# Seven block products for every two feed-forward units: the up-projections of a two-block float32 model as Strassen-Winograd products, with their outputs parked in DRAM

## The chip, the cores and the metric

The kernel is one program on one NeuronCore of a Trainium2 chip. The engines that matter are TensorE (PE in the profile), VectorE (DVE), ScalarE (ACT) and GpSimd (POOL); SyncE (SP) issues nearly all DMAs. The metric is the device time of one execution. Three runs of the kernel before took 3021.39 to 3023.06 us, median 3022.3 us.

## The reference

Two model blocks run one after the other on 1024 tokens of width 1024, all in float32. Each has a mixer part and then a feed-forward part with a residual sum. Only the feed-forward parts are changed:

```python
h = h + swiglu(rmsnorm(h, norm_ffn[i]), w_gate[i], w_up[i], w_down[i])   # first block, 2816 wide
#   swiglu: (silu(h @ w_gate) * (h @ w_up)) @ w_down
h = rmsnorm_2(x, g_ffn[i])                                               # second block, 4096 wide
x = x + jnp.square(jax.nn.relu(h @ w_ffn_up[i])) @ w_ffn_down[i]
```

The three matrices `w_gate`, `w_up` and `w_ffn_up` are the up-projections, `w_down` and `w_ffn_down` the down-projections. Below, FFN1 is the feed-forward part of the first block and FFN2 that of the second.

## The kernel before

**Numbers.** A float32 product is made of three TensorE products: each operand is split into a high part (a cast to fp32r, by ScalarE) and a low part (operand minus high part, by VectorE), and `mm3` (L139, L140, L141) adds high by high, high by low and low by high in PSUM. One such matmul has a 128x128 weight tile and 512 moving columns. The split is `split` (L103 ScalarE, L104 VectorE).

**Units.** 128 columns of an up-projection are a unit: 22 in FFN1, for gate and for up, and 32 in FFN2. The weights of a unit are one 512 KB tile, 128x1024: eight 128x128 tiles along the inner dimension k. Its output, 128 columns by 1024 tokens, fills one PSUM tile `big` of two banks, one for each half of the tokens; there are four of these tiles. A unit takes 8 k-tiles by 2 halves by 3 = 48 matmuls.

**Order of `ffn` (L639).** `norm_t` scales the residual rows and transposes them on TensorE (L192) into `hn`, 16 pairs of a high and a low half that stay in SBUF; `norm_units` does the first half of the tokens, starts the first units on it, and does the second half behind them. Then for each unit: product, activation (`swiglu` L664: Silu on ScalarE L667, product on VectorE L668; `relu2` L671: L674, L675), and the split of the result into `a` (L122, L124). After every third unit (four in FFN1's last chunk, two in FFN2's) `tok_matmul` multiplies the three `a` by their three rows of the down-projection, and VectorE adds each of the eight 128x1024 results to the residual tile (L659), which stays in SBUF. So up and down work alternate, and nothing of it goes through DRAM.

**What sets the order.** Each engine has one instruction stream, which a scheduler lays out when the program is built; an engine takes its instructions strictly in that order, and one that waits holds back all behind it. Tiles come from pools: 38 slots `S` of 128x1024 for all long-lived data, two buffers each for raw weights `wr`, split weights `wh` and `wl` and activations `zo`, and the four `big` in PSUM. The waits are made per tile: work on one half of a `big` tile waits for an earlier reader of its other half too.

## Time and profile before

| | us |
|---|---|
| median of three runs | 3022.3 |
| the profiled execution | 3025.18 |
| its span | 3023.3 |
| PE busy / DVE busy / ACT busy / POOL busy | 2899.8 / 1404.1 / 825.3 / 21.8 |

The span is the stretch in which the engines ran; the profiled execution is 1.9 us longer, and 2.9 us above the median of the runs. FFN1 begins with the transposes at 311.23 us and lasts until about 1050 us, FFN2 begins at 2191.8 us and lasts until 2917 us. Busy time of matmuls overlaps: a matmul is listed with 0.39 to 0.40 us and the next begins 0.23 us after its start, so the count of matmuls in a window says more than their sum.

### The profile page before, as it was taken

The numbers are of one execution on the slowest core, as the hardware profiler recorded it, in microseconds if no ns is written. First come the engines' busy times: TensorE is split into PE (matmuls) and PEld (weight loads), VectorE is DVE, ScalarE is ACT, GpSimd is POOL, SyncE is SP. The second block draws the span as 40 slices with busy tenths as digits, with TensorE's granted clock in tenths as the row PEclk, the third lists the DMA queues.
The fourth block names the chain that finished last, engine by engine and source line by source line (L and its number), as shares of the span: only waits on it lengthen the run. The fifth ranks groups of instructions, "written<-read, shape, count | busy, mean of one in ns | idle before, by whom it ended". The sixth has DMA issues, their size and how long they took to land.

```text
span 3023.3 us, 36716 instructions
## 1 busy us (share of the span) xinstructions
PE 2899.8 (96%) x15289; PEld 2327.6 (77%) x15289; DVE 1404.1 (46%) x2469; ACT 825.3 (27%) x1229; POOL 21.8 (1%) x73
## 2 busy tenths in 40 slices
PE   8989999999999999989788999999999999999998
PEld 6777888888888877867566777777888888888877
DVE  7774422222222462276676436545453333333366
ACT  4242311211121344143342334432131221111142
POOL 0000000000000000000000000000000000000000
PEclk9999999999999998999899999999999999999999
...
GB/s 133 105 128 146 35 42 42 63 44 40 42 63 49 73 137 153 105 117 90 69 90 88 98 83 13 29 105 134 75 35 42 42 56 49 56 49 42 42 77 98
DMA packets 126390, 225.37 MB, mean 75 GB/s; under 512 B 52177, under 2 KB 73297, under 8 KB 126225
## 3 DMA queue, kind: packets, MB, share of 16 engines
...
## 4 chain that ended last, share of the span: by engine, by line
PE 87%; DVE 9%; issue 2%; ACT 1%; DMA 1%; ACTq 0%; SPq 0%; DVEq 0%
PE big L139 24%; PE big L140 24%; PE big L141 24%; PE big L822 2%; PE chain L855 2%; DVE tt L1145 2%; DVE wt L1144 2%; PE ps L839 1%; PE ps L1114 1%; PE ps L1021 1%; PE big L192 1%; PE chain L1205 0%; PE chain L139 0%; PE chain L140 0%; PE chain L141 0%
## 5 line engine op out<-in xcount | busy, mean ns | idle before, releaser
L139 PE MATMUL big<-hn,wh 128*128 128x512 f32 x1872 | 745.6, 399 | 8.5 <-DVE zo L914 4.0
L141 PE MATMUL big<-hn,wl 128*128 128x512 f32 x1872 | 742.5, 397 | 5.3 <-DVE wl L104 5.2
L140 PE MATMUL big<-hn,wh 128*128 128x512 f32 x1872 | 744.5, 398 | 1.9 <-DVE hn L197 1.9
L139 PEld LDWEIGHTS big<-hn,wh 128*128 128x128 f32 x1872 | 352.8, 189 | 94.2 <-issue 6.2
L141 PEld LDWEIGHTS big<-hn,wl 128*128 128x128 f32 x1872 | 353.4, 189 | 90.7 <-DVE wl L104 8.4
L140 PEld LDWEIGHTS big<-hn,wh 128*128 128x128 f32 x1872 | 353.0, 189 | 88.0 <-issue 3.2
L103 ACT CAST wh<-wr 128x1024 fp32r<-128x1024 f32 (+1 forms) x142 | 141.9, 1000 | 966.4 <-PE big L140 777.4
L104 DVE TENSOR_TENSOR wl<-wr,wh 128x1024 fp32r<-128x1024 f32 (+1 forms) x142 | 165.0, 1162 | 410.5 <-ACT wh L103 405.7
L140 PE MATMUL big<-wk,a 128*128 128x512 f32 x864 | 338.4, 394 | 0.0
L141 PE MATMUL big<-wk,a 128*128 128x512 f32 x864 | 338.3, 393 | 0.0
L139 PE MATMUL big<-wk,a 128*128 128x512 f32 x864 | 334.9, 396 | 1.8 <-ACT wk L103 1.8
L659 DVE TENSOR_TENSOR r<-big,r 128x1024 f32<-128x1024 f32 x144 | 176.2, 1224 | 318.2 <-PE big L141 318.1
L139 PEld LDWEIGHTS big<-wk,a 128*128 128x128 f32 x864 | 160.9, 188 | 43.8 <-ACT wk L103 7.6
L140 PEld LDWEIGHTS big<-wk,a 128*128 128x128 f32 x864 | 162.2, 188 | 38.8 <-DVE wk L104 0.7
L141 PEld LDWEIGHTS big<-wk,a 128*128 128x128 f32 x864 | 162.2, 188 | 37.6
L674 ACT ACTIVATE zo<-big 128x1024 f32<-128x1024 f32 x32 | 32.8, 1026 | 371.4 <-PE big L141 371.4
L668 DVE TENSOR_TENSOR zo<-zo,big 128x1024 f32<-128x1024 f32 x22 | 26.9, 1221 | 205.2 <-PE big L141 205.2
L104 DVE TENSOR_TENSOR wk<-wr,wk 128x1024 fp32r<-128x1024 f32 (+1 forms) x86 | 100.3, 1171 | 31.1 <-ACT wk L103 31.0
L140 PE MATMUL big<-wk,mx 128*128 128x512 f32 x256 | 102.3, 399 | 1.3 <-DVE wk L104 1.3
L139 PE MATMUL big<-wk,mx 128*128 128x512 f32 x256 | 101.0, 401 | 2.3 <-ACT wk L103 2.3
L141 PE MATMUL big<-wk,mx 128*128 128x512 f32 x256 | 101.6, 397 | 0.0
L675 DVE TENSOR_TENSOR zo<-zo 128x1024 f32<-128x1024 f32 x32 | 39.2, 1225 | 131.7 <-ACT zo L674 131.7
...
## 6 DMA issues: line engine op xcount, KB each, us to landing
wr<-in_w_ffn_up_dram SPq DMA_DIRECT2D x32, 512.0 KB, 3.2
wr<-in_w_ffn_down_dram SPq DMA_DIRECT2D x32, 512.0 KB, 3.2
zr<-zo SPq DMA_DIRECT2D x24, 512.0 KB, 3.5
wr<-in_w_gate_dram SPq DMA_DIRECT2D x22, 512.0 KB, 3.3
wr<-in_w_up_dram SPq DMA_DIRECT2D x22, 512.0 KB, 3.2
wr<-in_w_down_dram SPq DMA_DIRECT2D x22, 512.0 KB, 3.2
wr<-in_w_gates_dram SPq DMA_DIRECT2D x16, 512.0 KB, 4.9
gd<-zo SPq DMA_DIRECT2D x16, 512.0 KB, 3.0
```

Of the source, the lines that this page charges most:

```text
L103: nc.scalar.copy(hi, x)
L104: nc.vector.tensor_tensor(lo, x, hi.bitcast(F32), ALU.subtract)
L139: nc.tensor.matmul(ps, lhsT=w[0], rhs=x[0], start=start, stop=False)
L140: nc.tensor.matmul(ps, lhsT=w[0], rhs=x[1], start=False, stop=False)
L141: nc.tensor.matmul(ps, lhsT=w[1], rhs=x[0], start=False, stop=stop)
L659: nc.vector.tensor_tensor(res[t], ps, res[t], ALU.add)
L674: nc.scalar.activation(s, ps, AF.Relu)
L675: nc.vector.tensor_tensor(s, s, s, ALU.mult)
L822: nc.tensor.matmul(sc[:, c:c + m], lhsT=qs[e][:, i * P:(i + 1) * P], rhs=ks[e][:, c:c + m], start=True, stop=True)
L855: nc.tensor.matmul(o, lhsT=pts[t // 4][:, (t % 4) * P:(t % 4 + 1) * P], rhs=vh, start=t == 0, stop=t == i)
L1144: nc.vector.tensor_tensor(t3, d[h, j:j + 1, j + 1:32].to_broadcast([64, n, m]), tt[h, 0:n, j:j + 1].to_broadcast([64, n, m]), ALU.mult)
L1145: nc.vector.tensor_tensor(tt[h, 0:n, j + 1:32], tt[h, 0:n, j + 1:32], t3, ALU.add)
```

## The change

For every two units j and j+1 of an up-projection, call the k-tiles 0 to 3 and 4 to 7 of their weights A11, A12 (unit j) and A21, A22 (unit j+1), and the two halves of k by the two halves of the tokens of the normed input B11, B12, B21, B22. The Strassen-Winograd scheme makes the four output blocks from seven products of four k-tiles each, 7 x 4 x 3 = 84 matmuls where two units took 96.

- `norm_blocks` makes B11, B21, B22 and the sums T1 to T4 of the input blocks, each split in high and low parts, once per feed-forward part; they stay in 28 of the 38 slots.
- `pair_weights` loads two units, makes the sums S1 to S4 of the weights with four GpSimd additions, and splits A11 with A12, S1 with S2, S3 with S4, and A22.
- `pair_steps` does the seven products in halves of two `big` tiles; p1, p5, u2 and u3 are partial sums in SBUF, and three copies on ScalarE, four additions on VectorE and one on GpSimd combine them.
- `ffn` does all pairs first, with the activation of each written to a DRAM tensor `hd`, and the residual to `rd`; afterwards it loads the residual, the activations and the down-projection again and does all chunks of the down-projection one after the other (a first chunk of one unit in FFN1, of two in FFN2, then three each: eight chunks for seven, and eleven as before).

```diff
+    def norm_blocks(self, res, g, groups=(3, 1)):
+        nc = self.nc
+        x = {n: [None] * 4 for n in ("B11", "B21", "B22", "T1", "T2", "T3", "T4")}
+        plain = [None] * 4
+        def norm_half(half):
+            xs, t = [], 4 * half
+            for n in groups:
+                xs += self.scaled(res[t:t + n])
+                t += n
+            for k in range(4):
+                ps = self.big()
+                for j in range(2):
+                    for i in range(4):
+                        c = (4 * j + i) * P
+                        nc.tensor.transpose(ps[:, c:c + P], xs[i][:, (k + 4 * j) * P:(k + 4 * j + 1) * P], self.ident)
+                p1, p2 = self.halves(ps)
+                g1, g2 = self.col(g, k), self.col(g, k + 4)
+                if half == 0:
+                    plain[k] = self.slot("bf")
+                    for n, p, c, f in (("B11", p1, g1, plain[k][:, 0:H]), ("B21", p2, g2, plain[k][:, H:2 * H])):
+                        x[n][k] = hi, lo = self.half_pair("hn")
+                        nc.scalar.activation(hi, p, AF.Identity, scale=c)
+                        nc.vector.tensor_scalar(f, p, c, None, ALU.mult)
+                        nc.gpsimd.tensor_tensor(lo, f, hi.bitcast(F32), ALU.subtract)
+                    continue
+                b12, t12, t34 = self.slot("tf")[:, 0:H], self.slot("tf"), self.slot("tf")
+                t1, t2, t3, t4 = *self.halves(t12), *self.halves(t34)
+                nc.scalar.activation(b12, p1, AF.Identity, scale=g1)
+                nc.gpsimd.tensor_tensor(t1, b12, plain[k][:, 0:H], ALU.subtract)
+                x["B22"][k] = hi, lo = self.half_pair("hn")
+                nc.scalar.activation(hi, p2, AF.Identity, scale=g2)
+                nc.vector.scalar_tensor_tensor(lo, p2, g2, hi.bitcast(F32), ALU.mult, ALU.subtract)
+                nc.vector.scalar_tensor_tensor(t3, p2, g2, b12, ALU.mult, ALU.subtract)
+                nc.vector.scalar_tensor_tensor(t2, p2, g2, t1, ALU.mult, ALU.subtract)
+                nc.gpsimd.tensor_tensor(t4, plain[k][:, H:2 * H], t2, ALU.subtract)
+                for t, names in ((t12, ("T1", "T2")), (t34, ("T3", "T4"))):
+                    hi, lo = self.slot("hn", F32R), self.slot("hn", F32R)
+                    self.split(t, hi, lo)
+                    for n, h, l in zip(names, self.halves(hi), self.halves(lo)):
+                        x[n][k] = h, l
+        return x, norm_half
+    def pair_weights(self, src):
+        nc = self.nc
+        raw = [self.wp.tile([P, 1024], F32, tag="wr", name=self.nm("wr"), bufs=2) for _ in range(2)]
+        for r, s in zip(raw, src):
+            nc.sync.dma_start(r, s)
+        a11, a12, a21, a22 = *self.halves(raw[0]), *self.halves(raw[1])
+        w = {}
+        def put(x, *names):
+            hi, lo = self.slot("wc", F32R), self.slot("wc", F32R)
+            self.split(x, hi, lo)
+            for n, h, l in zip(names, self.halves(hi), self.halves(lo)):
+                w[n] = h, l
+        put(raw[0], "A11", "A12")
+        yield w
+        s12, s34 = (self.wp.tile([P, 1024], F32, tag=t, name=self.nm("ws"), bufs=2) for t in ("wh", "wl"))
+        s1, s2, s3, s4 = *self.halves(s12), *self.halves(s34)
+        nc.gpsimd.tensor_tensor(s1, a21, a22, ALU.add)
+        nc.gpsimd.tensor_tensor(s2, s1, a11, ALU.subtract)
+        put(s12, "S1", "S2")
+        nc.gpsimd.tensor_tensor(s3, a11, a21, ALU.subtract)
+        nc.gpsimd.tensor_tensor(s4, a12, s2, ALU.subtract)
+        put(s34, "S3", "S4")
+        w["A22"] = self.half_pair("wc")
+        self.split(a22, *w["A22"])
+        yield w
+    def pair_steps(self, weights, x, c1, c2):
+        nc = self.nc
+        def product(ps, a, b, start):
+            for k in range(4):
+                self.mm3(ps, tuple(v[:, k * P:(k + 1) * P] for v in w[a]), x[b][k], start and k == 0, k == 3, skip_group_check=True)
+        w = next(weights)
+        pa, pb = self.halves(self.big())
+        p1 = self.slot("pr")[:, 0:H]
+        product(pa, "A11", "B11", True)
+        nc.scalar.copy(p1, pa)
+        product(pb, "A12", "B21", True)
+        nc.vector.tensor_tensor(c1[:, 0:H], pb, p1, ALU.add)
+        yield
+        next(weights)
+        pc, pd = self.halves(self.big())
+        p5 = self.slot("pr")[:, 0:H]
+        u2, u3 = self.halves(self.slot("pr"))
+        product(pc, "S1", "T1", True)
+        nc.scalar.copy(p5, pc)
+        product(pa, "S2", "T2", False)
+        nc.scalar.copy(u2, pa)
+        product(pd, "S3", "T3", True)
+        nc.vector.tensor_tensor(u3, pd, u2, ALU.add)
+        product(pc, "S4", "B22", False)
+        nc.vector.tensor_tensor(c1[:, H:2 * H], pc, u2, ALU.add)
+        nc.gpsimd.tensor_tensor(c2[:, H:2 * H], u3, p5, ALU.add)
+        product(pd, "A22", "T4", False)
+        nc.vector.tensor_tensor(c2[:, 0:H], pd, u2, ALU.add)
+        yield
+    def ffn(self, res, g, nf, chunks, up, act, w_down, last=lambda: None):
+        nc = self.nc
+        rd = self.dp.tile([T, D], F32, name=self.nm("rd"))
+        hd = self.dp.tile([nf, P, T], F32, name=self.nm("hd"))
+        for t in range(8):
+            nc.sync.dma_start(rd[t * P:(t + 1) * P, :], res[t])
+        x, norm_half = self.norm_blocks(res, g)
+        norm_half(0)
+        for j in range(0, nf, 2):
+            outs = []
+            for i, u in enumerate(up):
+                w = self.pair_weights((u[j], u[j + 1]))
+                c = [self.zo() if i == 0 else self.slot("cu") for _ in range(2)]
+                outs.append(c)
+                st = self.pair_steps(w, x, *c)
+                if j == 0 and i == 0:
+                    next(st)
+                    norm_half(1)
+                for _ in st:
+                    pass
+            for i in range(2):
+                act(*(c[i] for c in outs))
+                nc.sync.dma_start(hd[j + i], outs[0][i])
+        res = self.load_res(rd)
+        f = 0
         for nch in chunks:
             acts, wd = [], []
             for _ in range(nch):
-                if first:
-                    ps, first = first[:nu], first[nu:]
-                else:
-                    ps = [self.unit_t(ws.pop() if ws else self.weights(u[f]), hn) for u in up]
-                acts.append(act(*ps))
+                h = self.weights(hd[f], keep=True)
+                acts.append([tuple(v[:, half * H:half * H + H] for v in h) for half in range(2)])
                 wd.append(self.weights(w_down[f * P:(f + 1) * P, :], keep=True))
                 f += 1
             def evac(t, ps):
                 nc.vector.tensor_tensor(res[t], ps, res[t], ALU.add)
-                if t == 3 and f == sum(chunks):
+                if t == 3 and f == nf:
                     last()
             self.tok_matmul(acts, wd, evac)
...
+    def swiglu(self, g, u):
+        nc = self.nc
+        nc.scalar.activation(g, g, AF.Silu)
+        nc.vector.tensor_tensor(g, g, u, ALU.mult)
+
+    def relu2(self, h):
+        self.nc.vector.scalar_tensor_tensor(h, h, 0.0, h, ALU.max, ALU.mult)
 
...
-        self.ffn(res, "norm_ffn", (3, 3, 3, 3, 3, 3, 4), (a["w_gate"], a["w_up"]), self.swiglu, a["w_down"], self.ple_inputs)
+        res = self.ffn(res, "norm_ffn", FF1, (1,) + (3,) * 7, (a["w_gate"], a["w_up"]), self.swiglu, a["w_down"], self.ple_inputs)
-        self.ffn(res, "g_ffn_2", (3,) * 10 + (2,), (a["w_ffn_up"],), self.relu2, a["w_ffn_down"])
+        res = self.ffn(res, "g_ffn_2", FF2, (2,) + (3,) * 10, (a["w_ffn_up"],), self.relu2, a["w_ffn_down"])
```

What stands in the engines' streams now, at three places. A row is line, operation, what it writes and reads; the number behind a name is the buffer's, and the bracket names the engine or DMA queue whose semaphore it waits for.

ScalarE in the middle of FFN1, before: one unit pair of gate and up, where `big` is the finished gate product, `wh` and `wk` are weights of later work, `zo` the activation and `a` its high half.

```order
L103 CAST wh_3952<-wr_3950 128x1024 [waits DMAHW2_49,PE_49,Activation_49]
L667 ACTIVATE zo_3935<-big_3831 128x1024 [waits PE_49]
L103 CAST wh_4007<-wr_4005 128x1024 [waits DMAHW3_49,DVE_49,PE_49]
L122 ACTIVATE a_3938<-zo_3935 128x512 [waits DVE_49]
L122 ACTIVATE a_3939<-zo_3935 128x512
L103 CAST wk_3946<-wr_3944 128x1024 [waits DMAHW1_49]
```

ScalarE at the same place now, from the end of the gate pair to the up pair (`big_2968` and `big_3013` hold the gate pair, `big_3092` and `big_3137` the up pair; `zo_2958` and `zo_2959` are the two gate outputs, `pr` the partial sums, `ws` and `ws_3121` the sums of weights).

```order
L739 COPY pr_3014<-big_3013 128x512 [waits DVE_49,PE_49,Activation_49]
L741 COPY pr_3015<-big_2968 128x512 [waits DVE_49,PE_49]
L103 CAST wc_3088<-wr_3084 128x1024 [waits DMAHW0_49,Activation_49]
L795 ACTIVATE zo_2958<-zo_2958 128x1024 [waits DMAHW1_49,DVE_49]
L795 ACTIVATE zo_2959<-zo_2959 128x1024 [waits DMAHW2_49,DVE_49,Pool_49]
L730 COPY pr_3093<-big_3092 128x512 [waits PE_49,Activation_49]
L103 CAST wc_3124<-ws_3120 128x1024
L103 CAST wc_3130<-ws_3121 128x1024 [waits Activation_49]
L103 CAST wc_3134<-wr_3085 128x512 [waits DMAHW3_49,Activation_49]
```

The evacuation of p1 of the up pair (`pr_3093`) stands behind the two Silus, the second of which waits for VectorE's and GpSimd's parts of the gate pair; the cast of the next weight sums (`wc_3124`) stands behind it.

TensorE in the same up pair: the end of the product S3 T3 in one half of `big_3137` (with `hn_2738`) and the beginning of S4 B22 in its other half (with `hn_2644`).

```order
L139 MATMUL big_3137<-hn_2738,wc_3130 128x512
L140 MATMUL big_3137<-hn_2739,wc_3130 128x512
L141 MATMUL big_3137<-hn_2738,wc_3131 128x512
L139 MATMUL big_3137<-hn_2644,wc_3130 128x512 [waits DVE_49]
L140 MATMUL big_3137<-hn_2644,wc_3130 128x512
L141 MATMUL big_3137<-hn_2644,wc_3131 128x512
```

The product S4 B22 waits for VectorE, which reads u3 out of the half that S3 T3 has just written, and nothing else stands between the two. Before, at the same place of the same engine, the next unit began in a tile of its own:

```order
L140 MATMUL big_4491<-hn_2592,wh_4487 128x512
L141 MATMUL big_4491<-hn_2592,wl_4488 128x512
L139 MATMUL big_4546<-hn_2422,wh_4542 128x512 [waits Activation_49]
L140 MATMUL big_4546<-hn_2422,wh_4542 128x512
L141 MATMUL big_4546<-hn_2422,wl_4543 128x512 [waits DVE_49]
```

Its waits are for the unit's own weights, high part and low part; no evacuation of the tile just written stands among them.

ScalarE at the start of FFN1, the second half of the tokens, before: the squares of the four residual tiles (`xs`), then one ScalarE row for each half tile of the transposed input.

```order
L171 ACTIVATE xs_2594,t_2593<-r_392_2184 128x1024 [waits DVE_49]
L171 ACTIVATE xs_2596,t_2593<-r_393_2185 128x1024 [waits DVE_49]
L171 ACTIVATE xs_2598,t_2593<-r_394_2186 128x1024 [waits DVE_49]
L171 ACTIVATE xs_2625,t_2624<-r_395_2187 128x1024 [waits DVE_49]
L195 ACTIVATE hn_2585<-big_2646,vec 128x512 [waits PE_49]
L195 ACTIVATE hn_2586<-big_2646,vec 128x512
L195 ACTIVATE hn_2587<-big_2659,vec 128x512 [waits PE_49]
L195 ACTIVATE hn_2588<-big_2659,vec 128x512
```

The same place now: the evacuation of the first product (`pr_2550`), the squares, and for each of four k blocks four rows, of which the third waits for VectorE (T2) and the fourth for GpSimd (T4). The first block stands in the first piece, the last block and the casts of the first weight sums (`ws_2742`, `ws_2743`) in the second.

```order
L730 COPY pr_2550<-big_2549 128x512 [waits PE_49]
L171 ACTIVATE xs_2578,t_2577<-r_392_2184 128x1024 [waits DMAHW5_49,Activation_49]
L171 ACTIVATE xs_2580,t_2577<-r_393_2185 128x1024 [waits DMAHW6_49,Activation_49]
L171 ACTIVATE xs_2582,t_2577<-r_394_2186 128x1024 [waits DMAHW7_49,Activation_49]
L171 ACTIVATE xs_2609,t_2608<-r_395_2187 128x1024
L676 ACTIVATE tf_2639<-big_2630,vec 128x512 [waits PE_49]
L679 ACTIVATE hn_2644<-big_2630,vec 128x512
L103 CAST hn_2650<-tf_2640 128x1024 [waits DVE_49]
L103 CAST hn_2654<-tf_2641 128x1024 [waits Pool_49]
```

and, eight rows on:

```order
L676 ACTIVATE tf_2723<-big_2714,vec 128x512 [waits PE_49]
L679 ACTIVATE hn_2728<-big_2714,vec 128x512
L103 CAST hn_2734<-tf_2724 128x1024 [waits DVE_49]
L103 CAST hn_2738<-tf_2725 128x1024 [waits Activation_49,Pool_49]
L103 CAST wc_2746<-ws_2742 128x1024 [waits Activation_49]
L103 CAST wc_2752<-ws_2743 128x1024 [waits Activation_49]
```

The cast of S1 and S2, without which the third product cannot start, stands behind all sixteen rows of the four blocks.

VectorE between the last pair of FFN1 and the down-projection, now: `zo_5245` is the last activation, `wk_5517` the low part of the first activation read back, `wk_5523` that of the first rows of the down-projection, and the two L1035 rows belong to later work and write the buffers `zo`.

```order
L796 TENSOR_TENSOR zo_5244<-zo_5244,cu_5368 128x1024 [waits DVE_49]
L748 TENSOR_TENSOR cu_5369<-big_5423,pr_5425 128x512 [waits PE_49]
L796 TENSOR_TENSOR zo_5245<-zo_5245,cu_5369 128x1024 [waits DVE_49,Pool_49]
L1035 MEMSET zo_7621 128x1 [waits DMAHW0_49]
L1035 MEMSET zo_7633 128x1 [waits DMAHW2_49,DVE_49]
L104 TENSOR_TENSOR wk_5517<-wr_5514,wk_5516 128x1024 [waits Activation_49]
L104 TENSOR_TENSOR wk_5523<-wr_5520,wk_5522 128x1024 [waits DMAHW3_49,Activation_49]
L787 TENSOR_TENSOR r_902_5498<-big_5526,r_902_5498 128x1024 [waits DMAHW4_49,PE_49]
L787 TENSOR_TENSOR r_903_5499<-big_5534,r_903_5499 128x1024 [waits DMAHW5_49,PE_49]
```

The two L1035 rows wait for DMA queues: for the write of the last two activations to DRAM, whose buffers they take over; the low part of the first activation stands behind them.

## Rows read from the trace of the kernel before

**Rows 1.** The page, part 1: busy us, share, instructions.

```profile
PE 2899.8 (96%) x15289; PEld 2327.6 (77%) x15289; DVE 1404.1 (46%) x2469; ACT 825.3 (27%) x1229; POOL 21.8 (1%) x73
```

**Rows 2.** Windows, FFN1 and FFN2: length, busy (count) by engine, clock, DMA, GB/s.

```profile
350.00:700.00 350.00, 350.00 (x1510) 282.94 (x1509) 96.95 (x92) 56.42 (x66) 0.00 (x0) 1.00 0.15 50
2250.00:2600.00 350.00, 349.98 (x1505) 281.64 (x1504) 128.28 (x119) 62.51 (x75) 0.00 (x0) 1.00 0.14 46
```

**Rows 3.** Windows over the start of FFN1 and of FFN2, same columns.

```profile
311.20:345.00 33.80, 32.90 (x174) 27.29 (x173) 20.61 (x46) 18.61 (x30) 0.00 (x0) 1.00 0.05 16
2191.80:2225.00 33.20, 32.29 (x170) 26.64 (x169) 21.86 (x47) 18.51 (x30) 0.00 (x0) 1.00 0.04 11
```

**Rows 4.** PE there: start us, us, engine, line, operation, count, idle before.

```profile
311.23 3.65 PE L192 MATMUL big<-cst,xs 128*128 128x128 f32 x32
315.15 0.47 PE L139 MATMUL big<-hn,wh 128*128 128x512 f32 x1 [0.27 <-DVE hn L197]
315.46 0.39 PE L140 MATMUL big<-hn,wh 128*128 128x512 f32 x1
```

**Rows 5.** Timeline: a last matmul, VectorE behind it; VectorE, TensorE behind it.

```profile
1303.98 0.69 DVE L1084 TENSOR_TENSOR bv<-ps,v 128x512 f32<-128x512 f32 x1 [1.24 <-PE ps L1002]
...
1304.73 1.09 PE L1098 MATMUL ps<-cst,v 128*64 128x64 f32 x29
...
2916.43 0.40 PE L141 MATMUL big<-wk,a 128*128 128x512 f32 x1
...
2916.87 1.23 DVE L659 TENSOR_TENSOR r<-big,r 128x1024 f32<-128x1024 f32 x1 [0.81 <-PE big L141]
```

**Rows 6.** Groups by shape, ScalarE: busy, mean ns, idle before and its releaser.

```profile
L103 ACT CAST wh<-wr 128x1024 fp32r<-128x1024 f32 x130 | 136.2, 1048 | 945.3 <-PE big L140 768.3 <-DMA wr<-in_w_ffn_up_dram 137.5 <-issue 24.0
...
L195 ACT ACTIVATE hn<-big,vec 128x512 fp32r<-128x512 f32 x64 | 38.6, 695 | 80.5 <-PE big L192 80.2
L171 ACT ACTIVATE xs<-r 128x1024 f32<-128x1024 f32 x32 | 33.8, 1070 | 51.1 <-DVE r L631 42.9 <-DVE r L659 8.1
...
L842 ACT COPY pts<-ps 128x512 f32<-128x512 f32 x40 | 23.1, 578 | 10.4 <-PE ps L839 10.4
L667 ACT ACTIVATE zo<-big 128x1024 f32<-128x1024 f32 x22 | 22.5, 1021 | 9.5 <-PE big L141 9.5
```

**Rows 7.** The same for VectorE.

```profile
L659 DVE TENSOR_TENSOR r<-big,r 128x1024 f32<-128x1024 f32 x144 | 176.2, 1224 | 318.2 <-PE big L141 318.1
L104 DVE TENSOR_TENSOR wl<-wr,wh 128x1024 fp32r<-128x1024 f32 x130 | 158.9, 1222 | 394.2 <-ACT wh L103 389.6 <-DMA t_wkv<-tt 4.0
...
L197 DVE SCALAR_TENSOR_TENSOR hn<-big,vec,hn 128x512 fp32r<-128x512 f32 x64 | 43.4, 744 | 19.5 <-ACT hn L195 16.5 <-PE big L192 3.0
...
L1084 DVE TENSOR_TENSOR bv<-ps,v 128x512 f32<-128x512 f32 x8 | 5.4, 688 | 3.7 <-PE ps L1002 3.7
```

**Rows 8.** The same for GpSimd.

```profile
L784 POOL COPY kh<-kpe 64x512 f32<-64x512 f32 x16 | 10.5, 665 | 287.1 <-DMA kpe<-rope 162.2 <-PE ps L839 74.0 <-PE chain L855 50.2
```

**Rows 9.** Timeline of VectorE in the second half of FFN1's norm.

```profile
320.17 0.17 DVE L146 TENSOR_SCALAR t<-t 128x3 f32<-128x3 f32 x1 [1.22 <-ACT xs L171]
...
324.96 0.75 DVE L180 TENSOR_SCALAR xs<-r,t 128x1024 f32<-128x1024 f32 x1
```

**Rows 10.** Timeline of PE: two idle stretches.

```profile
241.75 0.80 PE L139 MATMUL big<-yg,wh 128*128 128x512 f32 x1 [4.61 <-ACT wh L103]
...
2896.77 1.21 PE L139 MATMUL big<-wk,a 128*128 128x512 f32 x4 [1.80 <-ACT wk L103]
```

**Rows 11.** Windows after these two, columns as in Rows 2.

```profile
241.70:247.30 5.60, 5.55 (x13) 4.44 (x14) 2.45 (x2) 2.33 (x2) 0.00 (x0) 0.50 0.56 174
...
2896.70:2900.00 3.30, 3.18 (x13) 2.29 (x14) 2.36 (x2) 0.98 (x2) 0.00 (x0) 1.00 0.31 86
```

**Rows 12.** The page, part 6: KB of one, us to landing.

```profile
zr<-zo SPq DMA_DIRECT2D x24, 512.0 KB, 3.5
```

More of the change, by code (lines that the diff above doesn't have):

```diff
@@ L135, in weights, with mm3 @@
         return w
-    def mm3(self, ps, w, x, start, stop):
+    def mm3(self, ps, w, x, start, stop, **kw):
         nc = self.nc
-        nc.tensor.matmul(ps, lhsT=w[0], rhs=x[0], start=start, stop=False)
-        nc.tensor.matmul(ps, lhsT=w[0], rhs=x[1], start=False, stop=False)
-        nc.tensor.matmul(ps, lhsT=w[1], rhs=x[0], start=False, stop=stop)
+        nc.tensor.matmul(ps, lhsT=w[0], rhs=x[0], start=start, stop=False, **kw)
+        nc.tensor.matmul(ps, lhsT=w[0], rhs=x[1], start=False, stop=False, **kw)
+        nc.tensor.matmul(ps, lhsT=w[1], rhs=x[0], start=False, stop=stop, **kw)
     def rsqrt(self, ss, n, scale, eps):
@@ L637, in load_res @@
         return res
-    def ffn(self, res, g, chunks, up, act, w_down, last=lambda: None):
+    def norm_blocks(self, res, g, groups=(3, 1)):
         nc = self.nc
-        hn, norm_half = self.norm_t(res, g)
-        nu = len(up)
-        ws = [self.weights(up[i % nu][i // nu], keep=i > 1) for i in range(3)]
-        first = self.norm_units(norm_half, hn, ws[0:2])
-        f, ws = 0, ws[2:]
+        x = {n: [None] * 4 for n in ("B11", "B21", "B22", "T1", "T2", "T3", "T4")}
[37 more added lines that the diff above has]
+        return x, norm_half
@@ L659, in evac @@
                 nc.vector.tensor_tensor(res[t], ps, res[t], ALU.add)
[L660 removed]
+                if t == 3 and f == nf:
                     last()
             self.tok_matmul(acts, wd, evac)
[L664 removed]
+        return res
+    def swiglu(self, g, u):
         nc = self.nc
[L666 to L676 removed]
+        nc.scalar.activation(g, g, AF.Silu)
+        nc.vector.tensor_tensor(g, g, u, ALU.mult)
+    def relu2(self, h):
+        self.nc.vector.scalar_tensor_tensor(h, h, 0.0, h, ALU.max, ALU.mult)
     def zo(self, cols=T):
```

11 lines of the change are left out of this document (removed).

## The prediction

> **What bounds the kernel now.** I read the page first: TensorE is busy for 96% of the span, GpSimd for 1% [rows 1]. Then windows inside the two feed-forward parts, to see whether any wait is left: in 350 us of FFN1 TensorE issues 1510 matmuls without a gap at full granted clock, one every 350 / 1510 = 0.2318 us, and nearly the same in FFN2 [rows 2]. (The 0.397 us that a matmul is listed with is no measure of what its removal gives, since it overlaps the next.) So both parts are bound by the count of matmuls, except at their start: there FFN1 issues 174 PE instructions in 33.80 us, 64 of them transposes, so 110 matmuls worth 25.5 us and 8.3 us of overhead; FFN2 differs little [rows 3]. Last I looked for what a wait costs, since the change adds waits.
>
> **What the change removes.** FFN1 has 2 x 22 units of 48 matmuls, 2112, and now 22 pairs of 84, 1848; FFN2 1536 and now 1344. 456 fewer x 0.2318 = 105.7 us, if TensorE stays as dense. All else is whether it does.
>
> **The price of one wait.** VectorE starts 0.44 us after the start of the last matmul whose result it reads, and TensorE starts 0.06 us after VectorE's 0.69 us end [rows 5]. A copy of half a tile out of PSUM takes 0.58 us on ScalarE [rows 6], an addition 0.69 on VectorE [rows 7]. So the next matmul can start 1.08 us (ScalarE) or 1.19 us (VectorE) after the start of the last; 0.23 of it is that matmul's own slot, and the first one behind a wait takes 0.31 instead of 0.23 [rows 4]: 0.94 and 1.05 us are lost, less 0.23 for each matmul that the order puts in between. By the order, a product on one half of a tile waits for the reader of the other half, so these waits come within the tile.
>
> **The steady part of FFN1**, for one pair of gate and one of up, 168 matmuls, 38.94 us. In the gate pair: A12 B21 behind the copy p1, nothing between, 0.94; S4 B22 behind u3, four matmuls of the next pair between, and u3 queued behind a split, 0.25; A22 T4 0.03. In the up pair: p1 stands behind two Silus. The second needs the gate pair's last addition (0.44 + 0.69), then itself 1.02 and the copy 0.58 [rows 6], with handovers 2.88 us after that last matmul started; that matmul's slot and four more cover 1.16, so 1.72 + 0.09 = 1.8. After A12 B21 comes VectorE's addition (to 1.13 after) and then, queued behind it, the low part of S1 and S2, 1.22 [rows 7]; less five slots, 1.35. S4 B22 behind u3, nothing between: 1.05. A22 T4 0.03. Sum 5.45, cycle 44.4 us, where 192 matmuls took 192 x 0.2318 = 44.5. **FFN1 therefore gains almost nothing per cycle**; with some 10.5 cycles, 57 us of stalls.
>
> **The steady part of FFN2**: one pair per cycle, no activation on ScalarE in front of p1 (relu2 is now a single VectorE row): 0.94 + 0.25 + 0.03 = 1.2, so 20.7 us instead of 22.25; 15 cycles, 18 us of stalls.
>
> **The start of each part.** Counting from the first transpose: 32 transposes to 3.7 [rows 4]. The half tiles are then read by ScalarE and VectorE in turns, four blocks of some 2.2 us (two rows of 0.695, one of 0.69 and handovers), to 10.6; cast and low part of A11 to 12.1; A11 B11 to 14.6, A12 B21 to 18.3. The squares of the second half, before long done by then, now stand on ScalarE behind p1: 15.4 to 19.7, four of 1.07 [rows 6]; the reciprocal root and the scaling 5.5 more [rows 9]: 24.7; transposes to 26. Then the T sums. For one block of k: B12 0.70 on ScalarE, its high neighbour B22 0.70; VectorE's low part, T3 and T2, 0.744 each [rows 7], to 3.7; T4 on GpSimd to 4.9 (1.2 us, below); the cast of T3 and T4, 1.05, to 6.0, and only then does ScalarE begin the next block. Four blocks: 24 us, to 49.5; the cast of S1 and S2 stands behind them: 50.5. Three products later, at 59.5, 60 matmuls are done, worth 13.9: overhead 45.6, less the old 8.3 = 37.3 us more. TensorE stands still for 7, 7 and 24 us in it. After an idle stretch of 4.61 us the granted clock was 0.50, that is 1.2 GHz, for 5.6 us and 13 matmuls; after one of 1.80 us it stayed at 1.00 [rows 10, 11]. 13 matmuls at half the clock lose some 2.5 us; I add 4 per part for the last two restarts. The order in FFN2 is the same. **2 x 41.3 = 83 us.**
>
> **Between up and down.** From the start of the last up matmul: addition to 1.1, product of gate and up, 1.22, to 2.4, its write to DRAM 3.5 us [rows 12], 5.9. VectorE's next rows wait for that write, since they take over the buffer; behind them stand the low parts of the first activation (to 7.1) and of the first down rows (to 8.4). The first chunk has one unit, 48 matmuls, and eight additions of 1.22 [rows 7]: VectorE is busy with them to about 22. The low part of the second chunk's first down rows stands behind all eight (23.5), and its raw buffers turn over two at a time: load 3.5, cast 1.05, low part 1.22, twice more, 35. By then 76 matmuls are done, 17.6 us: 17 us lost. FFN2 starts its chunks with two units, so that more matmuls cover the same loads: I take 14. Sum 31. Before, the activations went on in SBUF, with no such gap but single waits such as the 1.80 us [rows 10].
>
> **GpSimd's additions** are the unknown; the trace has none. Bounds from rows: not under 0.69, what VectorE takes for a half tile of the same shape [rows 7]; for the upper end the only GpSimd row with an input, 0.665 for a copy of as many columns [rows 8], counted once for each input and once more for the output, 2.0. I take 1.2, near two copies. The T chain moves by 4 x (difference): -2 to +3 us a part. In the steady part a pair's raw buffers return after a load and five such rows; in FFN1 10.8 us are over for five rows (2.16 each) before the next pair is late, in FFN2 11.4 (2.3 each). Within the bounds they stay hidden.
>
> The Trainium skill (GPSIMD Engine Reference, 3.1 and 1) gives 4497 ns for such an addition of 2048 columns, by an estimate 1.12 us for 512, and says that the engine shares its way into SBUF with VectorE when the latter has two SBUF inputs, as every low part here has. No row here shows either; by the figure alone the sum would be the same, the sharing speaks for more.
>
> The remaining edits: the residual to DRAM and back is 16 transfers of 512 KB beside a DMA share of 0.15 [rows 2], hidden; the splits are 3.5 instead of 2 per pair, with all the rest some 16 us of VectorE in an FFN1 cycle of 44.
>
> **Sum**: -105.7 + 57 + 18 + 83 + 31 = +83 us on the profiled 3025.2 us, 3108; the median of the runs is 2.9 us lower: **3105 us**. Its own range, 3070 to 3145: each start +-8, the transitions +-8 each, a steady wait +-0.25 us each on about 100.
>
> **Rivals.**
> 1. *The clock falls at the steady waits too.* Up to four waits of 0.9 to 1.8 us per FFN1 cycle, one per FFN2 cycle. The 1.80 us row speaks against it [rows 10, 11], but these waits come in clusters. One fall per FFN1 cycle and one in two of FFN2, 2.5 us each: 18 x 2.5 = 45, 3150. The Trainium skill (TensorE: Matmul & The Clock Gate, on HAM oscillation) says that idle gaps between groups of matmuls can make the clock go back and forth; here no row in the feed-forward parts shows it.
> 2. *GpSimd becomes the bound.* If it and VectorE hold each other up so that an addition takes 3 us, past the 2.2 at which it decides: FFN1 5 x 0.84 = 4.2 us per pair for 21 pairs, FFN2 5 x 0.7 = 3.5 for 15, each T chain 10: +88 + 53 + 20, 3266.
> 3. *The starts and transitions are half as long* because reads of PSUM and the T chain overlap more than I drew: place, ScalarE's queue at the second half's norm. Half of 75 and 31 and a third of the stalls away: -53 - 25, 3027; still not faster. Faster is reached when starts, transitions and stalls together fall below 105.7 instead of 189; with the T chain of a block at VectorE's own 4.7 us, half-priced waits (40) and starts of 22 and transitions of 6 each: -105.7 + 96 = -10, 3012. For it speaks only that drawn handovers may be too long.
> 4. *The kernel does not change the count of matmuls*: excluded by the order, which has 456 fewer.
>
> **Chances.** The forecast with its own range 0.60; rival 1 0.14; rival 2 0.09; cheaper but still slower (3028 to 3070) 0.08; faster 0.06; no change 0.03. About 0.2%, 6 us, is what a measurement of this kernel can tell. Range 3045 to 3180 takes in rival 1 and leaves out rival 2 and the faster side: 0.15 to 0.2 outside. Slower 0.91.
>
> **What would show it.** TensorE in the profile after should have about 14833 instructions (15289 - 456); windows in FFN1 should show 168 matmuls in some 44.4 us and in FFN2 84 in 20.7; at each start some 45 us with 60 matmuls; a stall of 24 us released by ScalarE's cast of S1 and S2; idle before S4 B22 from VectorE, about 1 us each. I am wrong if FFN1 runs below 42 us per cycle, if an addition on GpSimd takes above 2.2 us, if the clock in the steady windows is below 0.95, or if the start of a part costs under 25 us more.

## The result and the profile after

The changed kernel takes 3115.88 us (median of four runs, 3114.75 to 3116.28) and the kernel before 3022.68 beside it: ratio 1.0308, 95% interval 1.029 to 1.0326, slower by 93 us. The profiled execution took 3116.28 us with a span of 3114.5, 91.2 more than before. The forecast was 3105 us, slower. Of all executions below, one of the four with the squares first took 4041.94 us, at a mean granted clock of 0.65, and is left out of that experiment's ratio.

Part 1 of the page after (engine, busy us, share, instructions), against [rows 1]:

```profile
PE 2845.0 (91%) x14833; PEld 2247.5 (72%) x14833; DVE 1618.4 (52%) x2675; ACT 924.7 (30%) x1349; POOL 341.9 (11%) x295
```

The count has fallen by 456, as the order said. TensorE lost 55 us of busy time and gained 146 of idle time (span less busy: 123.5 before, 269.5 now), while no other engine comes near the span. So the question is where TensorE waits. The two feed-forward parts in the kernel before, each from its first transpose to the first transpose of the next part (for FFN1 that takes in some 30 us of the work behind it; columns as in [rows 2]):

```profile
311.23:1080.69 769.46, 767.45 (x3346) 620.69 (x3344) 247.64 (x353) 156.31 (x203) 0.00 (x0) 1.00 0.17 59
2191.13:2916.67 725.54, 722.76 (x3138) 582.18 (x3136) 286.26 (x313) 150.65 (x191) 0.00 (x0) 1.00 0.15 48
```

and in the kernel after, followed by pieces of them: two cycles of FFN1, the two starts, the stretch between up and down in FFN1 and in FFN2, FFN2's steady part, FFN1's steady part, and the first matmuls behind the longest wait between up and down:

```profile
310.07:1137.75 827.68, 737.65 (x3081) 572.30 (x3080) 374.64 (x486) 234.97 (x302) 176.15 (x122) 0.97 0.25 88
2247.10:3007.90 760.80, 701.29 (x2945) 552.60 (x2944) 378.79 (x392) 177.24 (x218) 132.32 (x92) 0.96 0.28 98
...
406.56:450.94 44.38, 40.61 (x169) 30.93 (x169) 16.22 (x18) 12.24 (x17) 14.57 (x10) 1.00 0.20 71
450.94:495.32 44.38, 40.63 (x168) 30.93 (x169) 16.10 (x18) 12.25 (x17) 14.58 (x10) 1.00 0.20 71
310.07:406.55 96.48, 59.46 (x245) 45.02 (x243) 48.48 (x73) 37.57 (x52) 36.92 (x26) 0.79 0.11 39
2247.10:2321.80 74.70, 40.66 (x161) 30.92 (x159) 41.17 (x65) 29.12 (x42) 29.66 (x21) 0.70 0.10 35
846.97:900.00 53.03, 40.36 (x151) 30.82 (x152) 32.50 (x30) 11.52 (x11) 0.00 (x0) 0.90 0.51 178
2638.37:2690.00 51.63, 45.93 (x175) 36.10 (x176) 33.95 (x29) 13.63 (x13) 0.00 (x0) 0.87 0.53 183
2321.83:2634.00 312.17, 293.72 (x1224) 225.55 (x1224) 144.65 (x146) 77.12 (x105) 101.37 (x70) 1.00 0.28 104
...
406.56:805.00 398.44, 364.41 (x1507) 277.33 (x1508) 145.29 (x161) 109.56 (x143) 130.74 (x90) 1.00 0.20 72
...
857.65:864.00 6.35, 6.35 (x17) 5.05 (x18) 2.66 (x3) 2.10 (x2) 0.00 (x0) 0.59 0.60 243
```

FFN1 is 58.2 us longer and FFN2 35.3; together 93.5, where the span is 91.2 longer, so the rest of the program has hardly changed (2.3 us less). Each piece is read in the way of the prediction: its length less its matmuls at 0.2318 us.

| term | predicted | measured |
|---|---|---|
| matmuls | -105.7 | -105.7 (456 fewer) |
| FFN1 steady waits | 5.45 a cycle, 57 | (406.56 to 805: 398.44 - 1507 x 0.2318 = 49.1 in 9 cycles) 5.46, 57 |
| FFN2 steady waits | 1.2 a pair, 18 | (312.17 - 1224 x 0.2318 = 28.5 in 14.6 pairs) 1.95, 28.5 |
| starts | 41.3 and 41.3 | 40.7 and 42.6 |
| up to down | 17 and 14 | 18.0 and 11.1 |
| sum | +83 | +92 |

(A start: 96.48 - 181 x 0.2318 - 5.5 for one steady cycle in it - 8.3 of before = 40.7; FFN2's by the same way with 97 matmuls, 1.0 and 8.6. The 64 transposes are in the overhead, as in [rows 3]. The terms leave some 3 us of FFN1 and -2 of FFN2 open.)

The idle times of TensorE name the waits. Its longest at FFN1's start, those of one steady cycle, and the first between up and down (start, us, engine, line, operation, count, idle before and its releaser):

```profile
320.81 0.79 PE L139 MATMUL big<-hn,wc 128*128 128x512 f32 x1 [7.09 <-ACT wc L103]
...
335.05 5.57 PE L663 MATMUL big<-cst,xs 128*128 128x128 f32 x24 [4.03 <-DVE xs L180]
...
362.37 0.80 PE L139 MATMUL big<-hn,wc 128*128 128x512 f32 x1 [19.48 <-ACT wc L103]
...
427.98 0.50 PE L139 MATMUL big<-hn,wc 128*128 128x512 f32 x1 [1.46 <-ACT pr L730]
...
431.86 0.51 PE L139 MATMUL big<-hn,wc 128*128 128x512 f32 x1 [0.38 <-DVE cu L732]
...
433.00 0.50 PE L141 MATMUL big<-hn,wc 128*128 128x512 f32 x1 [0.40 <-DVE wc L104]
...
441.52 0.50 PE L139 MATMUL big<-hn,wc 128*128 128x512 f32 x1 [0.85 <-DVE pr L743]
...
450.94 0.50 PE L139 MATMUL big<-hn,wc 128*128 128x512 f32 x1 [0.68 <-ACT pr L730]
...
857.65 0.79 PE L140 MATMUL big<-wk,wk 128*128 128x512 f32 x1 [6.94 <-DVE wk L104]
```

The 19.48 us end with the cast of S1 and S2, 52.3 us after the first transpose (50.5 forecast). The releasers L730, L732 and L743 are the readers of half a `big`. The steady cycle is 44.38 us at a granted clock of 1.00 throughout.

The long idle of the start is the T chain. ScalarE there, columns the same:

```profile
338.31 0.69 ACT L676 ACTIVATE tf<-big,vec 128x512 f32<-128x512 f32 x1 [6.25 <-PE big L663]
338.89 0.68 ACT L679 ACTIVATE hn<-big,vec 128x512 fp32r<-128x512 f32 x1
341.71 1.05 ACT L103 CAST hn<-tf 128x1024 fp32r<-128x1024 f32 x1 [2.13 <-DVE tf L682]
343.12 1.04 ACT L103 CAST hn<-tf 128x1024 fp32r<-128x1024 f32 x1 [0.36 <-POOL tf L683]
344.07 0.68 ACT L676 ACTIVATE tf<-big,vec 128x512 f32<-128x512 f32 x1
```

One block of k takes 5.76 us (338.31 to 344.07; 6.0 forecast): in each block ScalarE waits 2.13 us for VectorE's T2 and 0.36 for GpSimd's T4 before it can cast them and go on to the next block.

Between up and down, VectorE and the queue that issues the DMAs:

```profile
852.02 0.06 DVE L1035 MEMSET zo<- 128x1 f32 x1
852.10 0.32 SPq L775 DMA_DIRECT2D hd<-zo  x1
...
855.23 0.06 DVE L1035 MEMSET zo<- 128x1 f32 x1 [3.15 <-DMA hd<-zo]
855.23 2.36 DVE L104 TENSOR_TENSOR wk<-wr,wk 128x1024 fp32r<-128x1024 f32 x2
```

VectorE stands for 3.15 us at a memset of one column until the write of the last activation has left its buffer. Behind it stand two low parts, and TensorE's 6.94 us end with them.

### The profile page after: what moved, and what is told of

Its sections match the earlier page's. It is cut to its first block, busy times and chain, and to the rows that moved or that the text cites. A ratio compares the mean times of both kernels' runs of the same rounds, so it can differ in the third digit from the quotient of the medians.

```text
span 3114.5 us, 37183 instructions
## 1 busy us (share of the span) xinstructions
PE 2845.0 (91%) x14833; PEld 2247.5 (72%) x14833; DVE 1618.4 (52%) x2675; ACT 924.7 (30%) x1349; POOL 341.9 (11%) x295
## 5 line engine op out<-in xcount | busy, mean ns | idle before, releaser
L139 PE MATMUL big<-hn,wc 128*128 128x512 f32 x1064 | 432.9, 412 | 104.3 <-ACT wc L103 53.2
L141 PE MATMUL big<-hn,wc 128*128 128x512 f32 x1064 | 420.5, 401 | 15.2 <-DVE wc L104 15.2
L140 PE MATMUL big<-hn,wc 128*128 128x512 f32 x1064 | 422.6, 397 | 0.0
L140 PE MATMUL big<-wk,wk 128*128 128x512 f32 x864 | 344.2, 398 | 11.3 <-DVE wk L104 11.3
L139 PE MATMUL big<-wk,wk 128*128 128x512 f32 x864 | 341.1, 398 | 7.0 <-ACT wk L103 6.4
L141 PE MATMUL big<-wk,wk 128*128 128x512 f32 x864 | 343.1, 397 | 0.0
L139 PEld LDWEIGHTS big<-hn,wc 128*128 128x128 f32 x1064 | 202.6, 190 | 190.6 <-ACT wc L103 54.2
L139 PE MATMUL big<-hn,wh 128*128 128x512 f32 x688 | 280.1, 408 | 9.4 <-DVE zo L1035 4.0
L141 PE MATMUL big<-hn,wl 128*128 128x512 f32 x688 | 277.1, 403 | 5.3 <-DVE wl L104 5.3
L140 PE MATMUL big<-hn,wh 128*128 128x512 f32 x688 | 278.7, 405 | 0.6 <-DVE hn L197 0.6
L103 ACT CAST wk<-wr 128x1024 fp32r<-128x1024 f32 (+1 forms) x138 | 139.1, 1024 | 456.7 <-PE big L140 205.3
L141 PEld LDWEIGHTS big<-hn,wc 128*128 128x128 f32 x1064 | 202.3, 190 | 75.2 <-DVE wc L104 28.5
L140 PEld LDWEIGHTS big<-hn,wc 128*128 128x128 f32 x1064 | 202.9, 191 | 41.7
L140 PEld LDWEIGHTS big<-wk,wk 128*128 128x128 f32 x864 | 164.2, 190 | 51.3 <-DVE wk L104 13.2
L139 PEld LDWEIGHTS big<-wk,wk 128*128 128x128 f32 x864 | 164.0, 190 | 47.3 <-ACT wk L103 8.0
L141 PEld LDWEIGHTS big<-wk,wk 128*128 128x128 f32 x864 | 164.5, 190 | 38.2
L104 DVE TENSOR_TENSOR wc<-wr,wc 128x1024 fp32r<-128x1024 f32 x76 | 88.8, 1169 | 151.8 <-ACT wc L103 151.8
L139 PEld LDWEIGHTS big<-hn,wh 128*128 128x128 f32 x688 | 131.4, 191 | 43.5 <-issue 5.5
L141 PEld LDWEIGHTS big<-hn,wl 128*128 128x128 f32 x688 | 131.2, 191 | 36.8 <-DVE wl L104 6.4
L140 PEld LDWEIGHTS big<-hn,wh 128*128 128x128 f32 x688 | 131.3, 191 | 34.5 <-issue 3.2
```

Of the source, the lines that this page charges most:

```text
L103: nc.scalar.copy(hi, x)
L104: nc.vector.tensor_tensor(lo, x, hi.bitcast(F32), ALU.subtract)
L139: nc.tensor.matmul(ps, lhsT=w[0], rhs=x[0], start=start, stop=False, **kw)
L140: nc.tensor.matmul(ps, lhsT=w[0], rhs=x[1], start=False, stop=False, **kw)
L141: nc.tensor.matmul(ps, lhsT=w[1], rhs=x[0], start=False, stop=stop, **kw)
```

## The experiments

The theory was the sum in the table: waits that come from two halves sharing a tile, a start set by VectorE's and ScalarE's queues, a gap between up and down. The rivals: the trip through DRAM is what costs; GpSimd's additions are what costs; the waits are in the scheme itself. The experiments first undo or take one part each, and then put together what they found. The kernel before, run beside them, took 3023.4, 3024.3 and 3024.4 us.

**Each half in a tile of its own.** With `pa` and `pb` in tiles of their own (each uses half of it), a product need not wait for the reader of another half.

```diff
-        pa, pb = self.halves(self.big())
+        pa, pb = self.big()[:, 0:H], self.big()[:, 0:H]
...
-        pc, pd = self.halves(self.big())
+        pc, pd = self.big()[:, 0:H], self.big()[:, 0:H]
```

> Each of the four products that are open at a time gets a PSUM tile of its own (half of it unused), so that no product waits for the reader of another product's half. Theory (waits inside a tile make the steady loss): FFN1's cycle loses the waits for p1 (0.94 and 1.8 us) and for u3 (0.25 and 1.05), 44.4 to about 40.4 us, 10.5 times; FFN2's pair loses 0.94 + 0.25, 15 times: 3116 - 42 - 17 = 3057 us, 3048 to 3068. Rival (the queues of ScalarE and VectorE set the pace, and the waits come back one instruction later): 3100 to 3116.

It took 3033.34 us, 1.0032 of before (1.0022 to 1.0042): 82 us come back. Its windows over a cycle and the two parts, and the one idle left in that cycle:

```profile
427.75:467.68 39.93, 39.11 (x169) 31.47 (x169) 18.39 (x19) 12.36 (x16) 14.56 (x10) 1.00 0.22 79
312.34:1090.40 778.06, 720.47 (x3081) 578.34 (x3079) 392.83 (x486) 236.18 (x302) 180.60 (x122) 0.97 0.27 93
2202.92:2930.41 727.49, 684.84 (x2946) 553.04 (x2945) 393.30 (x392) 177.20 (x218) 135.60 (x92) 0.97 0.30 102
```

```profile
467.68 0.51 PE L141 MATMUL big<-hn,wc 128*128 128x512 f32 x1 [0.82 <-DVE wc L104]
```

The cycle is 39.93 us, where 168 matmuls alone take 38.94. So the steady waits do not belong to the scheme: they come from the two halves of one tile. The edit gave 24 us more than expected: I had thought that the waits for low parts would stay, and in FFN2 they went too. FFN1 closes: -61.2 of matmuls + 41 at the start + 18 between up and down (both from the table) + 10.5 x 1.0 = +8; it is 8.6 longer than before. FFN2 is 33.3 us shorter than in the change, where the steady part had 28.5 of waits; most of the rest lies in its first and last pair, which that piece leaves out.

**No sums of weights.** The four GpSimd additions of each pair are left out, and the splits of S1 to S4 take raw weights instead; so the output blocks are not those of the reference.

```diff
...
-        nc.gpsimd.tensor_tensor(s1, a21, a22, ALU.add)
-        nc.gpsimd.tensor_tensor(s2, s1, a11, ALU.subtract)
-        put(s12, "S1", "S2")
-        nc.gpsimd.tensor_tensor(s3, a11, a21, ALU.subtract)
-        nc.gpsimd.tensor_tensor(s4, a12, s2, ALU.subtract)
-        put(s34, "S3", "S4")
+        put(raw[1], "S1", "S2")
+        put(raw[0], "S3", "S4")
```

> Leaves out the four weight sums of each pair: S1 to S4 are the raw weights, and GpSimd adds nothing there. Theory (an addition on GpSimd and a low part on VectorE hold each other up, which makes the 0.75 us waits for a low part in about 10 of FFN2's 15 pairs): 8 to 11 us less in FFN2, within 3 us in FFN1, 3104 to 3109. Rival (GpSimd is hidden): 3113 to 3118. Rival (GpSimd sets the pace of the pairs): under 3090.

It took 3101.5 us, 1.0255 (1.0234 to 1.0276), 2.5 us under the range expected: FFN2 is 12.1 us shorter than in the change, FFN1 4.2. In FFN2 every pair now takes 20.68 us with one idle, as the prediction had it:

```profile
2379.07 0.50 PE L139 MATMUL big<-hn,wc 128*128 128x512 f32 x1 [0.73 <-ACT pr L724]
```

So without GpSimd's sums 14 of the 93 us are gone (the interval of the ratio is some 6 us to either side), and the run shows where the missing 0.75 us per pair of FFN2 is. In the change, two such meetings of GpSimd and VectorE, and TensorE behind the first:

```profile
2352.51 1.30 POOL L712 TENSOR_TENSOR ws<-wr,wr 128x512 f32<-128x512 f32 x1
...
2353.76 1.30 POOL L710 TENSOR_TENSOR ws<-ws,wr 128x512 f32<-128x512 f32 x1
2353.85 2.29 DVE L104 TENSOR_TENSOR wc<-wr,wc 128x1024 fp32r<-128x1024 f32 x1 [5.75 <-ACT wc L103]
...
2355.14 2.13 POOL L713 TENSOR_TENSOR ws<-wr,ws 128x512 f32<-128x512 f32 x1
...
2356.19 0.51 PE L141 MATMUL big<-hn,wc 128*128 128x512 f32 x1 [0.75 <-DVE wc L104]
...
416.76 1.23 DVE L104 TENSOR_TENSOR wc<-wr,wc 128x1024 fp32r<-128x1024 f32 x1 [5.71 <-ACT wc L103]
...
416.78 2.36 POOL L710 TENSOR_TENSOR ws<-ws,wr 128x512 f32<-128x512 f32 x1
```

VectorE's low part has two SBUF inputs; alone it takes 1.22 us [rows 7]. It begins 0.09 us after a GpSimd addition did, and ends 1.08 us after that addition's end; the next addition begins 1.00 before the low part ends and takes 2.13 instead of 1.30. At 416.76 the low part begins first: it keeps its 1.23 us, and the addition that begins 0.02 later takes 2.36. In each case the later one lasts about its own time, counted from the other's end: they exclude each other. The Trainium skill (SBUF — State Buffer, "SBUF: two separate sides") says so: the port pair that GpSimd and such a VectorE operation share is locked for a whole instruction, and the loser waits. By that rule the low part costs up to one addition, 1.3 us, more; this case's rows agree, with 1.07. The prediction had given the sharing and no size. The meeting costs TensorE time only where a matmul waits for the low part: with tiles of their own FFN2's pairs have no such wait although low parts take up to 2.3 us there too, so the 14 us of this run and the 82 of the one before overlap.

**The change in FFN2 alone**; FFN1 keeps its old method.

```diff
...
-        res = self.ffn(res, "norm_ffn", FF1, (1,) + (3,) * 7, (a["w_gate"], a["w_up"]), self.swiglu, a["w_down"], self.ple_inputs)
+        self.ffn_old(res, "norm_ffn", (3, 3, 3, 3, 3, 3, 4), (a["w_gate"], a["w_up"]), self.swiglu_old, a["w_down"], self.ple_inputs)
```

> Only FFN2 is changed, FFN1 is that of before. Theory (the cost is a sum of the terms, each within its part): 3022.7 - 44.5 (192 matmuls) + 28 (waits in the pairs) + 42.6 (start) + 11 (between up and down) = 3060, 3056 to 3064, with the FFN2 stretch as long as in the full change. Rival (the two parts act on each other): outside that.

It took 3048.33 us, 1.008 (1.0064 to 1.0096), some 12 under what I expected and outside the range. Part of the miss is in FFN2 itself: 754.14 us, 28.6 over before where the same code in the whole change is 35.3 over. Only 4 of its 15 pairs, not 10, have the wait for the low part, and a pair with it takes 21.75 us where one without takes 20.68: six fewer make 6.4 of these 6.7 us. The code of the pairs is the same, so which of the two begins first is set by something outside it, perhaps by where the loads stand; that was not tested. The rest of the 12 was not taken apart.

**The trip through DRAM alone.** The old units and matmuls, with the activations and the residual through DRAM and the down-projection as in the change.

```diff
...
+            s = act(*ps)
+            nc.sync.dma_start(hd[j], s)
...
```

> Products as before (48 matmuls per unit), but all units first, their activations through DRAM, and then the down-projection, as in the change. Theory (the round through DRAM costs only the stretch between up and down, 18 us in FFN1 and 11 in FFN2): 3052 us, 3044 to 3060. Rival (the traffic itself slows the loads): 3070 or more. Rival (the gap comes from the pairs' own queues, not from the round through DRAM): 3023 to 3035.

It took 3016.74 us, 0.9977 (0.9968 to 0.9986): not 30 us slower but 7 faster. Its two parts:

```profile
308.95:1078.50 769.55, 767.53 (x3346) 621.59 (x3344) 256.40 (x339) 155.33 (x181) 0.00 (x0) 1.00 0.27 92
2189.37:2910.45 721.08, 720.18 (x3138) 583.96 (x3137) 278.55 (x281) 146.97 (x159) 0.00 (x0) 1.00 0.30 101
```

My theory that the trip makes the gap fell: FFN1 is as long as before, FFN2 4.5 shorter, at 1.6 and 2.1 times the bytes per second. Here 16 slots hold the input, and seven low parts for the down-projection are done before the last activation. In the change 28 slots do, and its trace shows two casts, those of the first chunk, done ahead and no low part. So the gap is not DRAM's. That it is a lack of room and an order in VectorE's queue is tested below for the raw buffers and the order; for the slots it is argued from these counts alone.

**The squares first.** The squares and scalings of both halves stand at the head of a part, so that they are not queued behind the first products.

```diff
+        early, t = [], 0
+        for n in groups + groups:
+            early += self.scaled(res[t:t + n])
+            t += n
...
+            xs = early[4 * half:4 * half + 4]
```

> The change with one edit: the squares, reciprocal roots and scaling of both halves of the tokens are made before the first half is transposed, so that the second half's no longer stand on ScalarE behind the first product's evacuation. Theory (the start is a chain through ScalarE's queue): the first product that needs the sums starts some 39 us after the first transpose instead of 52.3, 13 us in each part: 3116 - 26 = 3090, 3082 to 3100. Rival (ScalarE and VectorE are simply full in the start): under 6 us in all, 3110 to 3116.

It took 3111.46 us, 1.0284 (1.0265 to 1.0303): 4 us less than the change, not 26. Two rows of TensorE, the first product and S1 T1:

```profile
326.54 0.79 PE L139 MATMUL big<-hn,wc 128*128 128x512 f32 x1 [10.78 <-ACT wc L103]
...
359.87 0.79 PE L139 MATMUL big<-hn,wc 128*128 128x512 f32 x1 [19.53 <-ACT wc L103]
```

The first transpose is at 312.11: S1 T1 comes after 47.8 us (52.3 before this edit), but the first product after 14.4 (10.7). What was taken from behind the products went in front of them, and the second half's transposes still stood in TensorE's stream behind those products, the first six matmuls of which ran at a granted clock of 0.50 behind the 10.78 us. A queue was shortened that was not the only one.

**Room for the loads.** The idle tiles `wh` and `wl` serve as raw buffers in the down phase, six for two; the buffer that is written to DRAM last is no longer the one that VectorE's memset waits for.

```diff
-                c = [self.zo() if i == 0 else self.slot("cu") for _ in range(2)]
+                c = [self.zo() if i == len(up) - 1 else self.slot("cu") for _ in range(2)]
...
+                tag = ("wr", "wh", "wl")[f % 3]
+                h = self.weights(hd[f], keep=True, tag=tag)
...
```

> The change with one edit between up and down: what is loaded for the down-projection takes six raw buffers instead of two (those of the weight sums too), and in FFN1 the output of the gate lies in a slot and that of the up unit in the short-lived buffer, so that nothing on VectorE waits for the last write to DRAM. Theory (the gap is queueing and too few buffers, not the round through DRAM): FFN1's 18 us go to about 5, FFN2's 11 to about 5: 3116 - 19 = 3097, 3089 to 3105. Rival (landing of the last write and loading back set the gap): 3110 to 3118.

It took 3093.99 us, 1.0228 (1.0214 to 1.0242), 22 less than the change, as expected in sum: FFN1 21 us shorter, FFN2 3. The stretch between up and down in FFN1 and in FFN2, the one idle left in FFN1's, and the wait for p1 of an up pair, 1.46 us in the change:

```profile
835.59:888.60 53.01, 49.11 (x201) 39.53 (x202) 40.70 (x37) 12.12 (x12) 0.00 (x0) 0.94 0.61 212
2622.15:2674.00 51.85, 47.73 (x199) 37.97 (x200) 38.91 (x34) 13.36 (x13) 0.00 (x0) 0.97 0.68 235
```

```profile
843.25 0.80 PE L140 MATMUL big<-wk,wk 128*128 128x512 f32 x1 [3.89 <-DVE wk L104]
...
426.97 0.50 PE L139 MATMUL big<-hn,wc 128*128 128x512 f32 x1 [0.68 <-ACT pr L730]
```

Read as in the table, the stretches lose 6.4 and 5.7 us, where the change loses 18.0 and 11.1: 17 of the 29 us come back. In FFN2, where the order of the buffers is not changed, the six raw buffers alone give 5.4 (its pairs, with other meetings of GpSimd and VectorE, take part of it back); in FFN1 the two parts of the edit were not separated. The rest of FFN1's 21 us is a side effect that I had not expected: with the gate's output in a slot the second Silu is done when the copy of p1 is due, TensorE waits 0.68 us for 1.46, and a cycle takes 43.6 us for 44.38. Why that Silu comes earlier was not followed up.

**All three**, and the splits of the T sums of one block moved behind the next block's reads, so that ScalarE does not wait in between.

```diff
+                late.append((k, t12, t34))
+                if k:
+                    splits(*late.pop(0))
```

> All edits together: own PSUM tile for each open product (e1), early squares (e5), six raw buffers (e6), and the splits of one block's sums written behind the next block's evacuations. Theory (the terms add): 3033 (e1) - 26 - 19 - 7 for the order of the splits = 2981, 2970 to 2995, clearly below before. Rival (what is taken from one wait goes to the next one, since ScalarE and VectorE fill up in the starts): 3005 or more.

It took 3003.09 us, 0.9933 (0.9921 to 0.9946), faster than before, but 22 us over what I expected: the start again gave less (S1 T1 at 44.8 us after the first transpose).

**The second half ahead of the first products.** What the squares' run had shown, mended: the first pair's weights are split first, and the second half's transposes and T sums stand before the first product.

```diff
+                if j == 0 and i == 0:
+                    w = chain([next(w)], w)
+                    norm_half(1)
...
-                if j == 0 and i == 0:
-                    next(st)
-                    norm_half(1)
```

> e7 with one more edit: the first two weight blocks are split right behind the first half's evacuations, and the second half's transposes and sums are written ahead of the first two products instead of behind them. It tests why e5 gave 4.5 us where 26 were expected. Theory (the second half's transposes stood in TensorE's stream behind the first products, which run at half clock, and the chain of sums could not start): the third product starts some 37 us after the first transpose instead of 44.8 in e7, 7 us less in each part: 3003 - 15 = 2988, 2981 to 2995. Rival (the sums are bound by VectorE's and ScalarE's work, wherever they start): 3000 to 3006.

It took 2988.43 us, 0.9887 (0.9869 to 0.9905), as expected: 36 us below the kernel before, 127 below the change. FFN1, the two starts, and TensorE's rows at the first product, at the next longest wait, and between up and down:

```profile
308.47:1059.66 751.19, 717.74 (x3082) 577.02 (x3080) 392.04 (x474) 230.59 (x296) 184.03 (x122) 0.98 0.28 97
...
308.47:390.62 82.15, 61.12 (x263) 48.68 (x261) 52.94 (x64) 36.49 (x48) 41.42 (x26) 0.83 0.15 52
2169.84:2230.00 60.16, 39.95 (x175) 31.85 (x174) 44.12 (x55) 27.88 (x38) 33.05 (x21) 0.80 0.15 53
```

```profile
327.86 0.77 PE L140 MATMUL big<-hn,wc 128*128 128x512 f32 x1 [3.93 <-DVE tf L693]
...
345.14 0.79 PE L140 MATMUL big<-hn,wc 128*128 128x512 f32 x1 [9.62 <-ACT wc L104]
...
787.77 0.79 PE L141 MATMUL big<-wk,wk 128*128 128x512 f32 x1 [3.89 <-DVE wk L105]
```

The wait of 19.48 us is down to 9.62, and ends 36.7 us after the first transpose. FFN1 is 18.3 us shorter than before; of the 61.2 that its matmuls give, 43 are still lost, most of it at the start: read as in the table, the starts lose some 27 and 26 us, where the change loses 40.7 and 42.6.

## Why the prediction was right, and which term was off

- **The gain of a matmul.** Right: 0.2318 us each. The run with own tiles shows it once the waits are gone, 39.93 us for 168.
- **FFN1's steady part.** Right to 0.01 us a cycle. The idle times shown, 3.77 in all, are less than what the waits cost: an idle time is counted from the end of the matmul before, 0.16 past its slot (431.09 + 0.23 to 431.86 is 0.54 where 0.38 is shown), and the first matmul behind it takes 0.1 longer, as the price of one wait had it. Counted so, the five rows give 5.07 of the 5.46; most of the rest is three steps of 0.11 us, too short to be listed as idle. The single waits came within 0.1 us of the forecast ones (0.94, 1.72, 1.30 and 1.11 for 0.94, 1.8, 1.35 and 1.05), so that the 0.01 of the sum is in part luck. Its source, the shared tile, is shown by the first experiment.
- **FFN2's steady part.** This term was mis-sized: 28.5 us for 18. The step that failed is "0.94 + 0.25 + 0.03 = 1.2": it took VectorE's low part at 1.22 us. In 10 of 15 pairs a GpSimd addition had begun just before it, the low part took 2.3 to 2.4, and the four matmuls of the next pair that were to fill the wait for u3 needed that low part. Such a pair took 1.07 us more, and ten of them are the miss. Without the additions every pair took 20.68 us, against 20.7 forecast.
- **GpSimd.** Taken at 1.2 us; it was 1.26 to 1.32 alone and up to 2.36 beside a VectorE operation. So one of the prediction's signs of being wrong came up: 16 of its 222 additions and subtractions took more than 2.2 us. What the sign stood for did not: the five rows of a pair took 1.46 us each on average (14.57 for ten in a cycle), and GpSimd was not the bound. Rival 2 had the mechanism, that it and VectorE hold each other up, but not the size. By the estimate from the Trainium skill (GPSIMD Engine Reference, 3.1) it would have been 1.12 us; the rows show 1.26 and more.
- **The starts.** Right in sum (41.3; 40.7 and 42.6). That is in part luck. Two stalls of the three were shorter than forecast: 7, 7 and 24 us, and 7.09, 4.03 and 19.48 measured, with 2.65 of short ones between. The clock took back part of that: in the 5.6 to 7.1 us behind the three stalls its mean was 0.57, 0.53 and 0.51, and the 24 transposes behind the second took 5.57 us at about half clock, where 32 of them took 3.65 at the start; the 4 us that the prediction gave to the clock were too few.
- **Between up and down.** 31 forecast, 29 measured. The prediction named the memset behind the write and the raw buffers as the cause, and the run that changes both gave 17 of it back. The plain trip through DRAM, with as many raw buffers and more slots, costs nothing.
- **Rival 1, the clock**, is excluded in the steady parts: 1.00 in the windows of both, with idles of up to 1.46 us. It fell where idles were long: behind the 6.94 us, 17 matmuls ran at a mean granted clock of 0.59. **Rival 3** needed halved starts and waits; the change has neither, but the last two runs, with the waits, the starts and the gaps cut down, came out faster than before. **Rival 4** is excluded by the count.
